# The FFN's gate and up projections as seven half-width block products

## The chip, the cores and the metric

The kernel runs on one core of one Trainium2 chip. The metric is the device time of one execution in microseconds (us). Timed executions are taken without the profiler; the profile is one further execution, taken with it. A core has a matrix engine (PE, with its weight loads shown as PEld), a vector engine (DVE), a scalar engine (ACT), a general engine (POOL, GpSimd) and a sync engine (SP) that issues most transfers. 16 DMA engines move the data. Matrix results land in PSUM, of which this kernel uses eight tiles of 128 partitions x 512 float32; all else on the core lies in SBUF.

## The reference

Two layers of a decoder trunk on x of 512 positions x 1024 channels, all in float32. A layer first mixes tokens (differential attention, retention and a gated short convolution, each projected, gated and summed, then an output projection). Its second half is the FFN:

```
h  = rmsnorm(x, norm_ffn_g)                 # 512 x 1024
gu = h @ w_ffn_in                           # 512 x 5632
g, u = gu[:, :2816], gu[:, 2816:]
g  = conv_b + sum over t = 0..2 of g shifted by 2 - t positions * conv_w[t]
x  = x + (silu(g) * u) @ w_ffn_out          # 2816 -> 1024
```

The FFN's 2816 inner channels are 22 tiles of 128.

## The kernel before, in words

Everything is held transposed: channels on the 128 partitions, the 512 positions along the free axis. x is eight tiles `x[k]` of 128 x 512.

**Three passes for one product.** Float32 operands are split into a high part, rounded to the format the matrix engine reads, and a low part, the rest. `mm3` multiplies hi x hi, hi x lo and lo x hi into one PSUM tile. Weights are split on arrival: `load_w` issues the transfer on SP's queue, `split_w` copies the high part on ACT and subtracts on DVE. Both stand in `tc.high_priority()` blocks.

**FFN.** `xg` are the splits of x times the norm's gain; the norm's factor per position, `rB`, is multiplied in after the product. For each tile f, `project` runs 8 k-blocks x 3 passes = 24 matmuls of 512 columns for g and 24 for u. DVE reads g from PSUM times `rB` into `pad`, `conv` makes the convolution with one ACT and two DVE instructions, silu is a Tanh on ACT and a DVE instruction, u is multiplied in, and `split2` makes `act[f]`. Tiles come in groups of 8, 7 and 7. After a group, eight rows d multiply its `act` tiles by `w2` (3 matmuls of 512 columns for each tile and row) and add to `x[d]`.

**Buffers.** Tiles of one tag share slots; a writer waits until an earlier tile of that slot has been read for the last time. Tag "N" has ten slots of 4 KB a partition: in the mixing part it holds values, queries, keys, normalised inputs and the branch inputs `om`; later it holds `y` and `act`. Tag "main" has four PSUM tiles for projections, "aux" four for the rest. `raw` has two slots; split weights of over 512 columns have three, of up to 512 two.

**Mixing part.** `head_chunk(h)` projects head h's q, k and v into the four "main" tiles; their evacuation writes `nat` and `v` (tag N). `attention(h)` turns `nat` into `q` and `k` (tag N) and runs scores, softmax and values through "aux". Gate projections (`side`) are interleaved with it by `weave`. `gate(0, d)` and `branch` follow, then `y` and the output projection.

**Order.** Each engine runs its queue in order. The program order is the order of the Python code; at build time a scheduler puts each engine's instructions in order by priority (program order, high-priority blocks first) on a simulated timeline, taking an instruction when its inputs and its slot are ready there.

Of the kernel before, what the change touches and what calls it, by code (L numbers as in the profile page):

```python
# [20 lines left out]
P = 128  # L21
# [8 lines left out]
GROUPS = (8, 7, 7)  # L30
# [8 lines left out]
FILL = 96  # L39
# [3 lines left out]
HL = 3  # L43

# [6 lines left out]
def trunk(ctx, tc, xT, wr, wh, wt, wda, wret, wsc, wo, wf, w2, par, lamp, relb, onehot, mask, rope, gtab, out):  # L51
# [6 lines left out]
    sp = ctx.enter_context(tc.tile_pool(name="sp", bufs=4))  # L58
    pm = ctx.enter_context(tc.tile_pool(name="pm", bufs=4, space=PSUM))
# [6 lines left out]
    def gslot(name):  # L66
        return tp.tile([P, S], F32, tag="g", name=name, bufs=9)

    def pairN(name):
        return tp.tile([P, 2, S], F32R, tag="N", name=name, bufs=10)  # L70

    def pairA(name, w=S):
        return tp.tile([P, 2, w], F32R, tag="aT", name=name, bufs=2, padded_shape=[P, 2, S])

    def wide(name, dt=F32R):
        return tp.tile([P, ST, 256], dt, tag="N", name=name, bufs=10)
# [33 lines left out]
    def main(name):  # L110
        return pm.tile([P, S], F32, tag="main", name=name)
# [6 lines left out]
    def ordered(i):  # L118

        if starting[0]:  # L120
            tc.keep_in_program_order(i)
        return i

    def load_w(src, name):
        n = src.shape[1]
        with tc.high_priority():
            raw = wp.tile([P, n], F32, tag="raw", bufs=2, name="raw_" + name, padded_shape=[P, D])
            ordered(nc.sync.dma_start(raw, src))
        return raw

    def split_w(raw, name):
        n = raw.shape[1]
        with tc.high_priority():
            tag, bufs = ("", HL) if 2 * n > D else ("b", 2)
            hi, lo = [
                wp.tile([P, n], F32R, tag=t + tag, name=f"{t}_{name}", padded_shape=[P, D if n > D // 2 else D // 2], bufs=bufs)
                for t in ("hi", "lo")
            ]
            A.copy(hi, raw)  # L139
            V.tensor_tensor(lo, raw, hi.bitcast(F32), ALU.subtract)  # L140
        return hi, lo
# [4 lines left out]
    def mm3(o, a, b, start, stop):  # L146

        T.matmul(o, a[0], b[0], start=start, stop=False)  # L148
        T.matmul(o, a[0], b[1], start=False, stop=False)  # L149
        T.matmul(o, a[1], b[0], start=False, stop=stop)  # L150
# [20 lines left out]
    xs = [cp.tile([P, 2, S], F32R, name=f"xs{k}") for k in range(KT)]  # L171
    klz = cp.tile([P, 2, S], F32R, name="klz")
    state = cp.tile([P, 2, ST - 1, P], F32R, name="state")
    qz = [cp.tile([P, ST, 2, P], F32R, name=f"qz{a}") for a in range(2)]
    rope_t = cp.tile([P, 2, ST, 64], F32, name="rope_t")
    mask_t = cp.tile([P, P], F32, name="mask_t")
    bias_t = cp.tile([P, H, S], F32, name="bias_t")
# [19 lines left out]
    def constants():  # L197
        for l in range(1, DEPTH):
            nc.sync.dma_start(pars[l], par[l])
        nc.sync.dma_start(gtab_t, gtab)  # L200
        nc.sync.dma_start(rope_t, rope)
        nc.sync.dma_start(mask_t, mask)

    def biases():

        rb = cp.tile([BUCKETS + 1, 16], F32, name="rb")[:, :H]
        V.memset(rb[BUCKETS : BUCKETS + 1], -BIG)
        G.dma_start(rb[:BUCKETS], relb)
        line = dr.tile([H, 640], F32, name="line")
        for a, b in ((0, 512), (512, 640)):  # L210
            oh = temp(f"oh{a}", b - a)[: BUCKETS + 1]
            G.dma_start(oh, onehot[:, a:b])
            ps = aux(f"psb{a}")
            T.matmul(ps[:H, : b - a], rb, oh, start=True, stop=True)
            row = temp(f"line{a}", b - a)[:H]
            V.tensor_copy(row, ps[:H, : b - a])
            G.dma_start(line[:, a:b], row)
        skew = dr.tile([H, P * 640], F32, name="skew")
        G.dma_start(skew.rearrange("h (p n) -> h p n", n=640), line.unsqueeze(1).broadcast_to([H, P, 640]))
        src = skew[:, 127 : 127 + 639 * P].rearrange("h (p n) -> p h n", n=639)  # L220
        G.dma_start(bias_t, src[:, :, :S])
# [5 lines left out]


    G.memset(state.bitcast(F32), 0.0)

    G.memset(klz.bitcast(F32), 0.0)
    for t in qz:
        G.memset(t.bitcast(F32), 0.0)
# [11 lines left out]
    def split_x(l, which, name, k):  # L245

        return split2(x[k], xs[k], pars[l][:, which + k : which + k + 1])
# [48 lines left out]
    def layer(l):  # L296
        pt = pars[l]
        L = f"L{l}"
        lam_init = 0.8 - 0.6 * math.exp(-0.3 * l)
# [56 lines left out]
        if not l:  # L356
            for _ in range(3 - STATS):
                next(first)
            constants()
        r, rB = norm_x(f"m{L}")  # L360
# [13 lines left out]
        if not l:  # L374
            biases()

# [52 lines left out]
        def attention(h):  # L429
# [22 lines left out]
            o = sp.tile([P, S], F32, tag="o", name=f"o{h}{L}", bufs=2)  # L452
# [265 lines left out]


        xg = [split_x(l, G_FFN, f"f{L}", k) for k in range(KT)]  # L720
        rB = None
        f0 = 0
        for grp, width in enumerate(GROUPS):
            act = []
            for fi in range(width):
                f = f0 + fi
                ps = main(f"pg{f}{L}")
                project(xg, ps, weights(wf[l, 2 * f], f"fg{L}{f}"))
                if rB is None:
                    _, rB = norm_x(f"f{L}")  # L730
                padt = pads[f % 2]
                V.tensor_tensor(padt[:, 2 : S + 2], ps, rB, ALU.mult)
                c = temp(f"c{f}{L}")
                wc = FF_W + 3 * f
                conv(c, padt, lambda t: pt[:, wc + t : wc + t + 1], pt[:, FF_B + f : FF_B + f + 1])
                th = temp(f"fth{f}{L}")
                A.activation(th, c, AF.Tanh, scale=0.5)
                V.scalar_tensor_tensor(c, th, 1.0, c, ALU.add, ALU.mult)
                ps = main(f"pu{f}{L}")
                project(xg, ps, weights(wf[l, 2 * f + 1], f"fu{L}{f}"))  # L740
                u = temp(f"u{f}{L}")
                V.tensor_tensor(u, ps, rB, ALU.mult)
                V.tensor_tensor(u, u, c, ALU.mult)
                at = pairN(f"act{f}{L}")
                act.append(split2(u, at))
            for d in range(KT):
                w = weights(w2[l, d, :, f0 * P : (f0 + width) * P], f"w2{L}{grp}{d}")
                ps = main(f"p2{grp}{d}{L}")
                project(act, ps, w)
                V.scalar_tensor_tensor(x[d], ps, 0.5, x[d], ALU.mult, ALU.add)  # L750
                if l == DEPTH - 1 and grp == len(GROUPS) - 1:
                    nc.sync.dma_start(out[:, d], x[d])
            f0 += width
# [37 lines left out]
def _layout(i):  # L791
# [28 lines left out]
    wf = i["w_ffn_in"].reshape(DEPTH, KT, P, 2, FT, P).transpose(0, 4, 3, 2, 1, 5)  # L820
    a["wf"] = C(wf).reshape(DEPTH, 2 * FT, P, KT * P)
# [40 lines left out]
```

## Time and profile before

| | |
|---|---|
| median of 3 runs | 1549.39 us (1548.54 to 1551.32) |
| the profiled execution | 1548.07 us |
| its span, first to last instruction | 1546.0 us |
| granted PE clock | 1.000 |
| PE busy | 1538.0 us |
| DVE busy | 980.2 us |
| ACT busy | 625.3 us |
| transfers | 147.04 MB |

The profile names a group of instructions by line, engine and operation, with output <- inputs; a number that tells tiles of one kind apart is left out of some names, and the last letter is the layer without its number, so one row often stands for both layers (x2: one in each). Shapes are partitions x elements. "Idle before" is the time the engine stood still ahead of the group, and what ended it. In the timeline a row begins with its start and its length in us. Matmuls are pipelined: one of 512 columns is shown 0.39 us long and the next starts sooner than that. The view of one tile gives shortest, median and longest duration in ns and the first and last start.

### The profile page before, as it was taken

How to read it: one execution, taken by the hardware profiler on the slowest of the kernel's cores; microseconds unless marked ns; L12 is line 12 of the kernel's file. 1: busy time of each engine (PE TensorE's matmuls, PEld its weight loads, DVE VectorE, ACT ScalarE, POOL GpSimd, SP SyncE). 2: the span in 40 equal slices, each digit the busy share in tenths (PEclk: the TensorE clock that was granted, in tenths of full speed). 3: DMA queues.
4: the chain of work that ended last, by engine and by line, in shares of the span. 5: the costliest groups of instructions: out<-in, count | busy, mean ns of one | idle time of the engine just before them, and what ended most of it. 6: DMA issues, size and time to landing. Idle time of an engine off the chain costs nothing.

```text
span 1546.0 us, 18968 instructions
## 1 busy us (share of the span) xinstructions
PE 1538.0 (99%) x7286; PEld 1304.6 (84%) x7286; DVE 980.2 (63%) x1826; ACT 625.3 (40%) x1057; POOL 10.0 (1%) x22
## 2 busy tenths in 40 slices
PE   9999999999999999999999999999999999999998
PEld 7899988888888888888889999888888888888887
DVE  8498886655576456456666887865555763664662
ACT  4456664333343233233425565643333432332331
POOL 1000000000000000000000000000000000000000
PEclk9999999999999999999999999999999999999999
DMA  5332222233233333332322222322323333323323
GB/s 188 120 99 71 76 93 96 75 103 89 96 96 96 96 100 93 97 105 91 100 82 93 72 89 73 96 76 91 101 95 94 96 97 96 96 89 102 96 89 102
DMA packets 46890, 147.04 MB, mean 95 GB/s; under 512 B 6119, under 2 KB 6518, under 8 KB 46800
## 3 DMA queue, kind: packets, MB, share of 16 engines
q1 hardware_dynamic: 45216, 143.11, 29.6%
q0 software_dynamic: 1584, 2.72, 0.6%
q8 instruction: 57, 0.93, 0.3%
q14 instruction: 33, 0.27, 0.1%
HBM read 143.70 MB, written 3.42 MB: 95 GB/s over the span
## 4 chain that ended last, share of the span: by engine, by line
PE 98%; DMA 1%; DVE 0%; ACT 0%; issue 0%; SPq 0%; ACTq 0%; DVEq 0%
PE pnrvgL L150 1%; PE pnrvgL L148 1%; PE pnrvgL L149 1%; PE pnrqkL L149 1%; PE pnrqkL L150 1%; PE pnrqkL L148 1%; PE pnh3L L149 1%; PE pnh1L L148 1%; PE pnh2L L150 1%; PE pnh3L L148 1%; PE pnh2L L148 1%; PE pnh1L L150 1%; PE pnh2L L149 1%; PE pnh1L L149 1%; PE pnh3L L150 1%; PE pnh0L L148 1%
## 5 line engine op out<-in xcount | busy, mean ns | idle before, releaser
L139 ACT CAST hi_tL<-raw_tL 128x1024 fp32r<-128x1024 f32 x60 | 63.0, 1050 | 124.5 <-DMA raw_tL<-in_wt 24.5
L139 ACT CAST hi_fuL<-raw_fuL 128x1024 fp32r<-128x1024 f32 x44 | 46.4, 1054 | 149.8 <-issue 17.5
L139 ACT CAST hi_w2L<-raw_w2L 128x896 fp32r<-128x896 f32 (+1 forms) x48 | 47.1, 982 | 139.8 <-PE p220L L149 11.8
L140 DVE TENSOR_TENSOR lo_tL<-raw_tL,hi_tL 128x1024 fp32r<-128x1024 f32 x60 | 73.4, 1224 | 16.8 <-ACT hi_tL L139 16.2
L139 ACT CAST hi_fgL<-raw_fgL 128x1024 fp32r<-128x1024 f32 x44 | 46.3, 1053 | 79.2 <-issue 13.0
L140 DVE TENSOR_TENSOR lo_fuL<-raw_fuL,hi_fuL 128x1024 fp32r<-128x1024 f32 x44 | 53.9, 1225 | 26.8 <-ACT hi_fuL L139 26.8
L140 DVE TENSOR_TENSOR lo_w2L<-raw_w2L,hi_w2L 128x896 fp32r<-128x896 f32 (+1 forms) x48 | 54.4, 1134 | 4.0 <-ACT hi_w2L L139 2.3
L140 DVE TENSOR_TENSOR lo_fgL<-raw_fgL,hi_fgL 128x1024 fp32r<-128x1024 f32 x44 | 53.7, 1220 | 3.5 <-ACT hi_fgL L139 3.5
L139 ACT CAST hi_oL<-raw_oL 128x1024 fp32r<-128x1024 f32 x16 | 16.9, 1054 | 56.4 <-PE ptg7L L149 13.1
L149 PE MATMUL pnrqkL<-lo_nrqkL,xs 128*128 128x512 f32 x64 | 25.2, 394 | 0.1
L150 PE MATMUL pnrvgL<-hi_nrvgL,xs 128*128 128x512 f32 x64 | 25.1, 392 | 0.0
L149 PE MATMUL pnrvgL<-lo_nrvgL,xs 128*128 128x512 f32 x64 | 25.0, 391 | 0.0
L150 PE MATMUL pnrqkL<-hi_nrqkL,xs 128*128 128x512 f32 x64 | 24.8, 390 | 0.0
L159 DVE SCALAR_TENSOR_TENSOR xs<-x,par,xs 128x512 fp32r<-128x512 f32 x32 | 23.9, 746 | 1.1 <-ACT xs L158 1.1
L148 PE MATMUL pnrqkL<-hi_nrqkL,xs 128*128 128x512 f32 x64 | 23.5, 403 | 0.9 <-ACT hi_nrqkL L139 0.9
L158 ACT ACTIVATE xs<-x,par 128x512 fp32r<-128x512 f32 x32 | 23.0, 718 | 3.0 <-DMA x<-in_xT 3.0
L148 PE MATMUL pnrvgL<-hi_nrvgL,xs 128*128 128x512 f32 x64 | 23.7, 394 | 0.0
L149 PE MATMUL pnh3L<-lo_nh3L,xs 128*128 128x384 f32 x64 | 22.1, 346 | 0.0
L140 DVE TENSOR_TENSOR lo_oL<-raw_oL,hi_oL 128x1024 fp32r<-128x1024 f32 x16 | 19.6, 1225 | 4.0 <-ACT hi_oL L139 4.0
L150 PE MATMUL pnh2L<-hi_nh2L,xs 128*128 128x384 f32 x64 | 21.9, 343 | 0.0
L149 PE MATMUL pnh2L<-lo_nh2L,xs 128*128 128x384 f32 x64 | 21.7, 339 | 0.0
L148 PE MATMUL pnh1L<-hi_nh1L,xs 128*128 128x384 f32 x64 | 21.7, 338 | 0.0
(3621 smaller groups left out, 5014.0 us busy)
## 6 DMA issues: line engine op xcount, KB each, us to landing
raw_tL<-in_wt SPq DMA_DIRECT2D x60, 512.0 KB, 3.6
raw_fgL<-in_wf SPq DMA_DIRECT2D x44, 512.0 KB, 3.5
raw_fuL<-in_wf SPq DMA_DIRECT2D x44, 512.0 KB, 3.5
raw_w2L<-in_w SPq DMA_DIRECT2D x32, 448.0 KB, 3.2
raw_oL<-in_wo SPq DMA_DIRECT2D x16, 512.0 KB, 3.6
raw_w2L<-in_w SPq DMA_DIRECT2D x16, 512.0 KB, 3.4
raw_nrvgL<-in_wr SPq DMA_DIRECT2D x8, 512.0 KB, 3.6
raw_bdL<-in_wda SPq DMA_DIRECT2D x16, 256.0 KB, 2.6
```

The lines of the kernel that those rows point to most:

```text
L139: A.copy(hi, raw)
L140: V.tensor_tensor(lo, raw, hi.bitcast(F32), ALU.subtract)
L148: T.matmul(o, a[0], b[0], start=start, stop=False)
L149: T.matmul(o, a[0], b[1], start=False, stop=False)
L150: T.matmul(o, a[1], b[0], start=False, stop=stop)
L158: A.activation(hi, src, AF.Copy, scale=g)
L159: V.scalar_tensor_tensor(lo, src, g, hi.bitcast(F32), ALU.mult, ALU.subtract)
```

## The change

The first group has five tiles and stays as it was but for silu, now one ACT instruction (`plain`); the other 17 tiles of a layer (groups of 9 and 8) go through `seven`. There g and u of one tile are a 2 x 2 block matrix: rows u and g, the two halves of the 1024 input channels as the inner blocks, the two halves of the positions as columns. Seven products of 4 k-blocks x 256 columns replace the eight that a plain computation has, with sums of weight blocks as one operand and sums of x blocks as the other.

The x side is made once per layer by `halves`: x times gain and `rB` for two of the eight k-tiles, two sums and two differences of their halves, and splits of seven blocks into `X[k]`. It is called after tiles 2, 3 and 4 and after row 1 of the first group. The weight side is made for each tile: `raw` holds blocks a11, a22 and a12; `s31` gets a fourth block twice by a transfer on SP, then a transfer on POOL's queue adds two other blocks to it; `s24` is two DVE adds. Splits of these go into `h31`, `l31`, `h24`, `l24`, four of the eight slots that hold `xg` in the first group (tag "x"), and into the weight slots (`w11`, `w2212`). The products share PSUM tiles a and b, which ACT and DVE read between products. Since X holds the norm, `seven` needs no `rB`. The convolution, silu and the product with u are as in `plain`.

Buffers: tag "N" has nine slots instead of ten; `raw` slots grow from 1024 to 1536 columns. Tables, gate slots and similar tiles of the mixing part lie in a pool that exists only there, X and the sums in one that exists only in the FFN, so `rope` and `bias` are loaded in each layer. In the group of nine a row's weights come in two pieces.

```diff
-GROUPS = (8, 7, 7)
+GROUPS = (5, 9, 8)
+HALF = S // 2
+NN = 9
...
     def pairN(name):
-        return tp.tile([P, 2, S], F32R, tag="N", name=name, bufs=10)
+        return tp.tile([P, 2, S], F32R, tag="N", name=name, bufs=NN)
...
+    def slotX(name):
+        return tp.tile([P, 2, S], F32R, tag="x", name=name, bufs=KT)
...
-            raw = wp.tile([P, n], F32, tag="raw", bufs=2, name="raw_" + name, padded_shape=[P, D])
+            raw = wp.tile([P, n], F32, tag="raw", bufs=2, name="raw_" + name, padded_shape=[P, 3 * S])
...
     def layer(l):
+        with tc.tile_pool(name=f"mix{l}", bufs=1, reuse_waits="tile", side="right") as mp:
+            phase[0] = mp
+            mix(l, mp)
+        with tc.tile_pool(name=f"ffn{l}", bufs=1, reuse_waits="tile", side="right") as fp:
+            ffn(l, fp)
...
+        def halves(k):
+            n = []
+            for j in (k, k + KT // 2):
+                t = temp(f"xn{j}{L}")
+                V.scalar_tensor_tensor(t, x[j], pt[:, G_FFN + j : G_FFN + j + 1], norm[0], ALU.mult, ALU.mult)
+                n.append(t)
+            b11, b12, b21, b22 = n[0][:, :HALF], n[0][:, HALF:], n[1][:, :HALF], n[1][:, HALF:]
+            t = sums4(f"xt{k}{L}")
+            V.tensor_tensor(t[:, 0], b11, b12, ALU.subtract)
+            V.scalar_tensor_tensor(t[:, 1], t[:, 0], -1.0, b22, ALU.mult, ALU.subtract)
+            V.tensor_tensor(t[:, 2], b22, b12, ALU.subtract)
+            V.scalar_tensor_tensor(t[:, 3], t[:, 1], -1.0, b21, ALU.mult, ALU.subtract)
+            flat = lambda a: a.rearrange("p a s -> p (a s)")
+            split(b11, X[k][:, 0, 0], X[k][:, 1, 0])
+            split(n[1], flat(X[k][:, 0, 1:3]), flat(X[k][:, 1, 1:3]))
+            split(flat(t), flat(X[k][:, 0, 3:7]), flat(X[k][:, 1, 3:7]))
...
+        def seven(f):
+            both = wf[l, f].rearrange("p (b n) -> p b n", n=S)
+            raw = load_w(wf[l, f, :, S:], f"f{L}{f}")
+            a11, a12 = raw[:, :S], raw[:, 2 * S :]
+            with tc.high_priority():
+                s31 = fp.tile([P, 2, S], F32, tag="sum", name=f"s31{f}{L}", bufs=3)
+                nc.sync.dma_start(s31, both[:, 0:1].broadcast_to([P, 2, S]))
+                G.dma_start(s31, both[:, 1:3], accum_op=ALU.add)
+                w11 = split_w(a11, f"fa{L}{f}")
+                h31, l31 = slotX(f"h31{f}{L}"), slotX(f"l31{f}{L}")
+                split(s31, h31, l31)
+                s24 = fp.tile([P, 2, S], F32, tag="sum", name=f"s24{f}{L}", bufs=3)
+                V.tensor_tensor(s24[:, 0], s31[:, 1], a11, ALU.add)
+                V.tensor_tensor(s24[:, 1], s24[:, 0], a12, ALU.add)
+                h24, l24 = slotX(f"h24{f}{L}"), slotX(f"l24{f}{L}")
+                split(s24, h24, l24)
+                w2212 = split_w(raw[:, S : 3 * S], f"fb{L}{f}")
...
+            def product(o, w, b, start, stop):
+                for k in range(KT // 2):
+                    sl = slice(k * P, (k + 1) * P)
+                    mm3(o, (w[0][:, sl], w[1][:, sl]), (X[k][:, 0, b], X[k][:, 1, b]), start and k == 0, stop and k == KT // 2 - 1, True)
+
+            a = main(f"pa{f}{L}")[:, :HALF]
+            b = main(f"pb{f}{L}")
+            padt = pads[f % 2]
+            u = temp(f"u{f}{L}")
+            product(a, w11, 0, True, True)
+            A.copy(padt[:, 2 : HALF + 2], a)
+            product(b[:, HALF:], (h31[:, 1], l31[:, 1]), 3, True, True)
+            A.copy(u[:, HALF:], b[:, HALF:])
+            product(a, (h24[:, 0], l24[:, 0]), 4, False, True)
+            A.copy(padt[:, HALF + 2 : S + 2], a)
+            product(b[:, HALF:], (h24[:, 1], l24[:, 1]), 2, False, True)
+            product(a, (h31[:, 0], l31[:, 0]), 5, False, True)
+            V.tensor_tensor(u[:, HALF:], u[:, HALF:], a, ALU.add)
+            product(b[:, :HALF], w12, 1, False, True)
+            V.tensor_tensor(padt[:, 2 : S + 2], padt[:, 2 : S + 2], b, ALU.add)
+            product(a, w22, 6, False, True)
+            A.copy(u[:, :HALF], a)
+            c = temp(f"c{f}{L}")
+            wc = FF_W + 3 * f
+            conv(c, padt, lambda t: pt[:, wc + t : wc + t + 1], pt[:, FF_B + f : FF_B + f + 1])
+            A.activation(c, c, AF.Silu)
+            V.tensor_tensor(u, u, c, ALU.mult)
+            return split2(u, pairN(f"act{f}{L}"))
...
+            for f in range(f0, f0 + width):
+                act.append(seven(f) if grp else plain(f))
+                if grp == 0 and f >= 2 and len(todo) > 1:
+                    halves(todo.pop(0))
             for d in range(KT):
+                rows(grp, f0, act, d)
+                if todo and d == 1:
+                    halves(todo.pop(0))
```

More of the change, by code (lines that the diff above doesn't have):

```diff
@@ L38 @@
 SINGLE = 1
-FILL = 96
+FILL = 80
 SOME = 5
@@ L144, in weights, with mm3 @@
         return split_w(load_w(src, name), name)
[L146 to L150, printed above, removed]
+    def mm3(o, a, b, start, stop, more=False):
+        T.matmul(o, a[0], b[0], start=start, stop=False, skip_group_check=more)
+        T.matmul(o, a[0], b[1], start=False, stop=False, skip_group_check=more)
+        T.matmul(o, a[1], b[0], start=False, stop=stop, skip_group_check=more)
     def split(src, hi, lo, g=None):
@@ L200, in constants @@
         nc.sync.dma_start(gtab_t, gtab)
-        nc.sync.dma_start(rope_t, rope)
         nc.sync.dma_start(mask_t, mask)
+    skew = dr.tile([H, P * 640], F32, name="skew")
     def biases():
@@ L296, in layer, with mix, tables @@
     def layer(l):
+        with tc.tile_pool(name=f"mix{l}", bufs=1, reuse_waits="tile", side="right") as mp:
[3 more added lines that the diff above has]
+            ffn(l, fp)
+    def mix(l, mp):
         pt = pars[l]
         L = f"L{l}"
+        klz = mp.tile([P, 2, S], F32R, name=f"klz{L}")
+        state = mp.tile([P, 2, ST - 1, P], F32R, name=f"state{L}")
+        qz = [mp.tile([P, ST, 2, P], F32R, name=f"qz{a}{L}") for a in range(2)]
+        rope_t = mp.tile([P, 2, ST, 64], F32, name=f"rope{L}")
+        bias_t = mp.tile([P, H, S], F32, name=f"bias{L}")
+        G.memset(state.bitcast(F32), 0.0)
+        G.memset(klz.bitcast(F32), 0.0)
+        for t in qz:
+            G.memset(t.bitcast(F32), 0.0)
+        def tables():
+            src = skew[:, 127 : 127 + 639 * P].rearrange("h (p n) -> p h n", n=639)
+            G.dma_start(bias_t, src[:, :, :S])
         lam_init = 0.8 - 0.6 * math.exp(-0.3 * l)
@@ L722, in layer @@
         f0 = 0
+        todo = list(range(KT // 2))
         for grp, width in enumerate(GROUPS):
             act = []
[L725 to L745, printed above, removed]
```

91 lines of the change are left out of this document (58 added, 33 removed).

## The prediction

> **What bounds the kernel now.** I read the page first, then the granted clock, then windows over one group of the feed-forward part (FFN).
>
> ```profile
> span 1546.0 us, 18968 instructions
> ...
> PE 1538.0 (99%) x7286; PEld 1304.6 (84%) x7286; DVE 980.2 (63%) x1826; ACT 625.3 (40%) x1057; POOL 10.0 (1%) x22
> ...
> PE 98%; DMA 1%; DVE 0%; ACT 0%; issue 0%; SPq 0%; ACTq 0%; DVEq 0%
> ```
>
> ```profile
> core 0: us, PE busy (x) PEld busy (x) DVE busy (x) ACT busy (x) POOL busy (x), PEclk, DMA share, GB/s
> 1318.00:1389.00 71.00, 71.00 (x314) 58.79 (x314) 46.63 (x59) 26.71 (x33) 0.00 (x0) 1.00 0.31 95
> 1389.00:1432.00 43.00, 43.00 (x191) 35.64 (x190) 17.48 (x20) 9.46 (x10) 0.00 (x0) 1.00 0.33 98
> ```
>
> The chain that ended last is 98% PE, and in both stages of a group (the first window makes `act` tiles, the second multiplies them by `w2`) PE is busy all the time at full clock, with no wait left to remove. So only less PE work shortens this kernel, and any wait that the change puts on PE is paid in full. A busy PE says nothing about its rate; for that I take steps from start to start.
>
> ```profile
> L148 PE MATMUL pg9L<-xs,hi_fgL x16: 389/389/389, 559.2 to 1328.9; 128*128 128x512 f32 x16
> ...
> L148 PE MATMUL pg10L<-xs,hi_fgL x16: 389/389/389, 570.1 to 1339.8; 128*128 128x512 f32 x16
> ```
>
> ```profile
> 1320.55 0.39 PE L150 MATMUL pu8L<-xs,lo_fuL 128*128 128x512 f32 x1
> 1320.55 0.19 PEld L148 LDWEIGHTS pu8L<-xs,hi_fuL 128*128 128x128 f32 x1
> 1320.78 0.39 PE L148 MATMUL pu8L<-xs,hi_fuL 128*128 128x512 f32 x1
> ```
>
> ```profile
> 73.71 0.28 PE L148 MATMUL pS01L<-qz,rT2L 128*128 128x256 f32 x1
> ...
> 74.31 0.28 PE L150 MATMUL pS01L<-qz,rT2L 128*128 128x256 f32 x1
> ```
>
> One FFN tile (g and u, 48 matmuls of 512 columns) takes 570.1 - 559.2 = 10.9 us, 0.227 us a matmul. The retention scores are six matmuls of 256 columns in a row: (74.31 - 73.71) / 5 = 0.120 us a step. So half the width costs 53% of the time, and each step has about 13 ns that don't shrink (2 x 0.120 - 0.227).
>
> **The change, part by part.** Five of the 22 tiles of a layer stay plain; 17 become seven products.
>
> *PE, seven products.* Each is 4 k-blocks x 3 passes = 12 matmuls of 256 columns, so a tile is 84 x 0.120 = 10.08 us instead of 48 x 0.227 = 10.88: 0.80 us less, 34 tiles in two layers, **-27.2 us**. The 12.5% fewer columns become 7%, since the 13 ns come 84 times instead of 48. That 0.120 holds for a long run, too, rests on the weight load: four transposes of 128 columns, each with a load of its own, take 0.44 us, 110 ns each,
>
> ```profile
> 169.44 0.44 PE pto0L L288 x4
> ```
>
> so loads can follow each other at least that fast, just under 120. Between 0.110 and 0.125 a step the term is -55 to -13 us; I take 0.120, measured at this width. The `w2` matmuls keep their number and width.
>
> *Vector and scalar work per tile.* The nearest rows:
>
> ```profile
> L140 DVE TENSOR_TENSOR lo_fgL<-raw_fgL,hi_fgL 128x1024 fp32r<-128x1024 f32 x44 | 53.7, 1220 | 3.5 <-ACT hi_fgL L139 3.5
> L139 ACT CAST hi_fgL<-raw_fgL 128x1024 fp32r<-128x1024 f32 x44 | 46.3, 1053 | 79.2 <-issue 13.0
> ```
>
> ```profile
> L139 ACT CAST hi_bdL<-raw_bdL x16: 604/623/624, 294.1 to 1121.5; 128x512 fp32r<-128x512 f32 x16
> L140 DVE TENSOR_TENSOR lo_bdL<-raw_bdL,hi_bdL x16: 682/684/685, 295.4 to 1122.3; 128x512 fp32r<-128x512 f32 x16
> ```
>
> ```profile
> L600 ACT COPY onr1L<-por11L x2: 374/374/374, 113.6 to 878.5; 128x256 f32<-128x256 f32 x2
> L601 DVE TENSOR_TENSOR onr1L<-onr1L,por11L x2: 420/421/422, 114.0 to 878.9; 128x256 f32<-128x256 f32 x2
> ```
>
> ```profile
> L294 DVE SCALAR_TENSOR_TENSOR c9L<-pad,par,c9L 128x512 f32<-128x512 f32 x1 | 0.8, 753 | 0.0
> ...
> L743 DVE TENSOR_TENSOR u8L<-u8L,c8L 128x512 f32<-128x512 f32 x1 | 0.7, 693 | 0.0
> ```
>
> ```profile
> L292 ACT ACTIVATE c9L<-pad,par 128x512 f32<-128x512 f32 x1 | 0.8, 812 | 0.0
> ...
> L737 ACT ACTIVATE fth9L<-c9L 128x512 f32<-128x512 f32 x1 | 0.6, 631 | 2.0 <-DVE c9L L294 2.0
> ```
>
> DVE: low part of `w11` 0.68; of `s31`, `s24` and `w2212` 3 x 1.22; the two adds for `s24` 2 x 0.69; `u+=a` 0.42; `pad+=b` 0.69; the convolution 2 x 0.75; `u*c` 0.69; low part of `act` 0.68. Sum 9.70 us in 10.08, where the window above has 46.63 / 71.00 of it. ACT: 0.62 + 3 x 1.05 + four PSUM copies 4 x 0.37 + 0.81 + Silu (not in the trace; 0.63 as the Tanh) + 0.62 = 7.31 us. DVE fits, because independent instructions overlap:
>
> ```profile
> 1319.80 1.22 DVE L140 TENSOR_TENSOR lo_fuL<-raw_fuL,hi_fuL 128x1024 fp32r<-128x1024 f32 x1 [0.17 <-ACT hi_fuL L139]
> 1320.94 0.74 DVE L293 SCALAR_TENSOR_TENSOR c8L<-pad,par,c8L 128x512 f32<-128x512 f32 x1
> ```
>
> 1.22 long, but the next starts after 1.14; eight such pairs bring 9.70 to about 9.1. That lies beside PE, with 1 us to spare per tile, and two tiles' worth of weight slots as a cushion. On average it costs nothing; if the cover were gone (PE waiting for all of DVE's surplus) the price is the last rival.
>
> *Hand-offs inside a tile.* All seven products go through two PSUM tiles, so PE waits at four places for a reader: products 3, 4 and 5 for ACT copies, product 7 for DVE's `u+=a`. Between comes one product, 12 x 0.120 = 1.44 us. A result lands 0.28 - 0.12 = 0.16 us after its step, the copy is 0.37 (DVE 0.42): about 0.8 us remain for whatever stands ahead on the engine, and that is a weight split of 1.05 (ACT) or 1.22 (DVE) marked high priority. Bounds: nothing, if no split stands in front; (1.22 - 0.8) + 3 x (1.05 - 0.8) = 1.2 us if one does each time. Big splits fill 3.15 / 10.08 of ACT's time and only the first quarter of each hurts, so nearer to nothing: 0.1 us a tile, **+3.4 us** (0 to 40).
>
> *Ten N slots become nine.* The mixing phase before the FFN uses all ten. From the views of single tiles:
>
> ```profile
> L155 ACT CAST oms0L<-scy0L x2: 612/612/612, 106.6 to 870.8; 128x512 fp32r<-128x512 f32 x2
> ...
> L148 PE MATMUL pb22L<-oms0L,hi_b2L x2: 402/402/402, 205.6 to 970.6; 128*128 128x512 f32 x2
> ```
>
> ```profile
> L158 ACT ACTIVATE om0L<-pto0L,par x2: 689/689/689, 169.9 to 934.9; 128x512 fp32r<-128x512 f32 x2
> ```
>
> ```profile
> L501 PE MATMUL po22L<-v2L,aT23L x8: 330/332/338, 232.4 to 998.2; 128*128 128x256 f32 x8
> ```
>
> ```profile
> L158 ACT ACTIVATE v3L<-pnh3L,rmL x8: 366/370/390, 202.6 to 971.6; 128x128 fp32r<-128x128 f32 x8
> ```
>
> ```profile
> L465 PE MATMUL pS022L<-k2L,q2L x2: 427/427/427, 204.8 to 969.8; 128*128 128x384 f32 x2
> ...
> L465 PE MATMUL pS123L<-k2L,q2L x2: 448/448/448, 216.3 to 981.3; 128*128 128x512 f32 x2
> ```
>
> At 203 us the branch inputs `oms0`, `oms1`, `omr0`, `omr1` are held, `om0` too, head 2's `v2`, `q2`, `k2`, and `nat3`; `v3` is the tenth. With nine it can't be written until `q2` and `k2` are free, at 216.3 in this order. Until then all four main PSUM tiles hold head 3's projection, and the gate projections queued behind it on PE stop. Bounds per layer: 0, if another slot is free by then, to 216.3 - 204.8 = 11.5 us. Without the gates PE reaches the last scores of head 2 sooner, so I take 3 us a layer, **+6 us**. The other full stretches delay only attention tiles that gate matmuls cover.
>
> *Group ends and starts.* The first `w2` row needs the group's last `act` at once: with eight in a group PE has 21 matmuls (4.8 us) before it, with five only 12 (2.7 us). The plain tail behind PE is 0.69 + 0.69 + 0.62 + 0.68 = 2.7 us and some gaps; the seven-product tail is longer (0.37 or 0.69, 0.81, 1.50, 0.63, 0.69, 0.62, 0.68, part of it under product 7: some 4 us against 5.4 or 4.8 of cover), and the next tiles' splits (5.7 us of DVE) push in with priority. `halves` adds some 5.6 us of DVE four times in the first group. Bounds 0 to 5 us a layer; **+3.4 us** for both layers together.
>
> *Transfers.* Per tile 768 KB of weights, 512 KB for `s31`, and 512 KB that add to it, 1.8 MB against 1.0.
>
> ```profile
> raw_fgL<-in_wf SPq DMA_DIRECT2D x44, 512.0 KB, 3.5
> ...
> bias_t<-skew POOLq DMA_DIRECT2D x1, 1024.0 KB, 5.8
> skew<-line POOLq DMA_DIRECT2D x1, 1280.0 KB, 19.4
> ```
>
> Share 0.31 now, so 0.6 of the 16 engines, and 0.75 if adding doubles its half MB. No row has an adding transfer: between 3.5 us (a plain one) and 19.4 us (the slowest of POOL's); I take 6. It waits for the plain transfer on POOL's queue, where in the FFN nothing stands behind it. 3.5 + 6 us end well inside the two tiles (20 us) by which `s31` can run ahead: 0 on the path. What POOL's queue gets besides (a second bias load, memsets) comes tens of us before use: 0, as do the second `rope` load on SP and the strided plain weights.
>
> *Sum* against the profiled execution (1548.07, span 1546.0 and 2.1 around): -27.2 + 3.4 + 6 + 3.4 = -14.4. The median of the runs is 1.3 above that execution; from it, 1549.4 - 14.4 = **1535 us**.
>
> **The rivals.**
>
> *Full gain.* Waits and slots cost nothing: 1549.4 - 27.2 = 1522. For it: PE has no idle stretch today, and queues are ordered for readiness. Against it: 9.1 us of DVE in 10.08, and the tenth slot in use.
>
> *Slower: DVE and ACT as the pace of the seven products.* Place: the four hand-offs. If queues put one big split before each and DVE, late, pushes the next tile's splits into the next hand-offs, a tile loses the 1.2 us above: 34 x 1.2 = 41, with the other terms 1549.4 - 27.2 + 41 + 9 = 1572. It decides from (27.2 - 9.4) / 34 = 0.52 us a tile upwards. For it: DVE goes from 66% to over 90%. Against it: ACT has a quarter of its time free.
>
> *No change.* Slots at their upper bound (23 us for both layers) and hand-offs as forecast: 1549.4 - 27.2 + 23 + 3.4 = 1549.
>
> *Adding transfers set the pace.* `s31` and `s24` share three buffers; with about 5 us for `s24` and 5 for the splits, an adding transfer above some 17 us ((3.5 + 17 + 5 + 5) / 3 = 10.2) makes `s31` late. At 19.4 a tile takes (3.5 + 19.4 + 5 + 5) / 3 = 11.0 us, 0.9 more: 1549.4 - 14.4 + 34 x 0.9 = 1566.
>
> *A weight load that doesn't overlap.* Then each half-width matmul would take 0.110 + 0.120 and a tile 84 x 0.23 = 19.3 us: 1549.4 + 34 x 8.4 = 1835. The rows speak against it: the load at 1320.55 starts together with a matmul, and the step is 0.227, not 0.110 longer. The Trainium skill, "TensorE: Matmul & The Clock Gate", in the part on packing small matmuls ("The mechanism"), says that a weight load overlaps matmuls in flight only when their row group differs; by that rule this rival would be the forecast, and this trace does not agree.
>
> **How the numbers follow.** Forecast 0.52 (1527 to 1544), full gain 0.16, no change 0.10, DVE and ACT 0.18, adding transfers 0.03, load 0.01. The range for 8 in 10 leaves out the upper part of the slower cases: 1521 to 1558. Less than 0.2% (3.1 us) can't be told from none here. Faster: 0.52 + 0.16 and a part of the no-change case, 0.70; same, the rest of that case, 0.08; slower 0.18 + 0.03 + 0.01 = 0.22.
>
> **What would show it.** Seven-product tiles with 84 matmuls, 10.1 us from tile to tile when undisturbed; a step near 0.120. Gaps on PE ahead of products 3, 4, 5, 7, ended by ACT copies or `u+=a`; a gap near 205 and 970 us ended by `v3`; gaps at the first `w2` row. DVE above 85% in those windows, DMA share near 0.6, and adding transfers that land in under 10 us. Wrong would be: a step above 0.125, tiles above 10.6 us, PE waiting for `h31`, or no gap at `v3`.

## The result, and the profile after

| | before | after |
|---|---|---|
| median of the runs | 1549.18 us (1548.54 to 1551.32) | 1636.78 us (1630.98 to 1642.64) |
| the profiled execution | 1548.07 us | 1636.98 us |
| span | 1546.0 us | 1635.2 us |

The ratio is 1.0563, 95% interval 1.0542 to 1.0584: slower by 5.6%. The forecast was 1535 us, and the time lies far outside its range.

From the page of after: the span, PE's busy time, the granted clock in 40 slices, the DMA share in the same slices, and the chain of work that ended last.

```profile
span 1635.2 us, 22053 instructions
...
PE 1556.4 (95%) x8510; PEld 1369.2 (84%) x8510; DVE 1066.0 (65%) x2006; ACT 734.6 (45%) x1304; POOL 43.2 (3%) x61
...
PEclk9999989999999999989999999999999999998899
DMA  5422212232225752652422222222323366426623
...
PE 73%; DMA 12%; DVE 7%; issue 5%; ACT 3%; SPq 0%; POOLq 0%; ACTq 0%; DVEq 0%
```

The chain that was 98% PE now runs through transfers for 12% and DVE for 7%. PE's own time splits the loss. Idle PE went from 1546.0 - 1538.0 = 8.0 us to 1635.2 - 1556.4 = 78.8 us: 70.8 more. Busy PE grew by 18.4 us although the products should have taken 27.2 off it: 45.6 more for the same matmuls. The mean granted clock of after is 0.973, and 0.027 x 1635 = 44 us of clock are missing, though some of the half-clock time is idle time too. So of the 70.8 + 45.6 = 116.4 us lost (27.2 of them made good by the products) some 60% is waiting, and most of the rest is PE running at half clock after it waited.

By stage, from windows of after (span, busy time and count of each engine, granted clock, DMA share, GB/s; the stages are mixing, plain tiles, their `w2` rows, the group of nine with its rows, the group of eight with its rows) and, below, of before (mixing and FFN). Layer 0 alone is shown; in layer 1 the mixing stage loses 11.2 us and the FFN some 7 us more than here, in the same stages.

```profile
6.00:427.60 421.60, 412.79 (x2039) 353.75 (x2039) 284.99 (x654) 196.05 (x391) 4.61 (x7) 0.99 0.30 97
427.60:483.40 55.80, 55.80 (x253) 46.33 (x252) 41.71 (x70) 26.32 (x34) 0.00 (x0) 1.00 0.25 82
483.40:516.40 33.00, 29.40 (x121) 23.09 (x121) 24.95 (x40) 13.09 (x19) 0.92 (x1) 0.95 0.49 138
516.40:672.10 155.70, 145.78 (x973) 136.09 (x972) 98.42 (x133) 70.60 (x115) 8.49 (x10) 0.97 0.54 143
672.10:817.80 145.70, 132.31 (x865) 122.32 (x864) 91.27 (x121) 68.00 (x107) 9.25 (x11) 0.94 0.46 126
```

```profile
6.00:416.30 410.30, 407.55 (x2039) 351.60 (x2039) 286.90 (x654) 197.32 (x391) 4.59 (x7) 1.00 0.32 100
416.30:776.80 360.50, 360.50 (x1598) 298.58 (x1596) 211.48 (x273) 123.19 (x151) 0.00 (x0) 1.00 0.31 96
```

The mixing stage is 421.6 - 410.3 = 11.3 us longer. The FFN takes 390.2 us instead of 360.5 (817.8 - 427.6), where 346.9 were expected (17 tiles x 0.80 us less): 43 us too many, in the two groups of seven-product tiles and the rows ahead of them. The plain tiles are undisturbed.

What PE waits for in 672 to 775 us of after, and what DVE waits for in 505 to 775 us (us in total, times, longest). DVE's first row is twelve waits for splits of `w2`, the longest 3.7 us; the rows behind it are the adds for `s24`:

```profile
PE pa14L L159 <- DVE u14L L828: 6.0, 1, 6.0
PE pa19L L159 <- DVE pad L830: 2.7, 1, 2.7
PE pa20L L159 <- DVE pad L830: 1.9, 1, 1.9
```

```profile
DVE lo_w2L L151 <- ACT hi_w2L L150: 18.4, 12, 3.7
DVE s2417L L804 <- DMA s3117L<-in_wf: 6.6, 1, 6.6
DVE s2420L L804 <- issue: 5.6, 1, 5.6
DVE s2416L L804 <- DMA s3116L<-in_wf: 5.2, 1, 5.2
```

PE waits for DVE to read a PSUM tile, but DVE is not busy: it waits for an adding transfer. (For tile 20 the profile names no releaser; the adding transfer is issued at 724.0 us and lands 6.8 us later, when the wait ends.) DVE's queue in order of time shows the rest:

```profile
686.84 1.22 DVE L167 TENSOR_TENSOR l3116L<-s3116L,h3116L 128x1024 fp32r<-128x1024 f32 x1
687.97 0.68 DVE L830 TENSOR_TENSOR pad<-pad,pb14L 128x512 f32<-128x512 f32 x1
695.24 0.69 DVE L804 TENSOR_TENSOR s2417L<-s3117L,raw_fL 128x512 f32<-128x512 f32 x1 [6.58 <-DMA s3117L<-in_wf]
695.85 0.41 DVE L828 TENSOR_TENSOR u14L<-u14L,pa14L 128x256 f32<-128x256 f32 x1
```

The next product on PE is the seventh of tile 14, and it needs `u14 += a`. But the first add for `s24` of tile 17 stands in DVE's queue *ahead of* that read. The add waits 6.58 us for its transfer; the 0.41 us read behind it waits as long. The same on ACT puts a split of `s31` of tile 5 ahead of the splits of `w2` at 489 us (it waits 6.53 us), which lengthens the rows of the first group.

The transfer is late because its chain begins late. The two issues for tile 17, on SP and on POOL, and the instruction that releases the first:

```profile
676.25 1.22 DVE L167 TENSOR_TENSOR l2415L<-s2415L,h2415L 128x1024 fp32r<-128x1024 f32 x1
```

```profile
677.50 0.38 SPq L798 DMA_DIRECT2D s3117L<-in_wf  x1
```

```profile
685.88 0.85 POOL L799 DMA_DIRECT2D s3117L<-in_wf  x1 [9.14 <-DVE lo_faL L151]
```

With three "sum" buffers and two a tile, `s31` of tile f takes the buffer of `s24` of tile f - 2. The transfer starts when that is split (676.25 + 1.22 = 677.47). The first transfer lands 7.8 us after its issue (the row of the second names a DVE instruction that ends shortly after), the second 9.3 after its own, and the sum is there 17.7 us after the start, at 695.2. These two are the slowest pair of the 17 tiles; the medians are 5.7 and 7.0. With the splits the next release, `l2417`, comes 28.2 us after `l2415`, where two tiles of PE's work are 20.2.

### The profile page after: what moved, and what is told of

It is laid out like the page before. It is cut to its first block, busy times and chain, and to the rows that moved or that the text cites. A ratio compares the mean times of both kernels' runs of the same rounds, so it can differ in the third digit from the quotient of the medians.

```text
span 1635.2 us, 22053 instructions
## 1 busy us (share of the span) xinstructions
PE 1556.4 (95%) x8510; PEld 1369.2 (84%) x8510; DVE 1066.0 (65%) x2006; ACT 734.6 (45%) x1304; POOL 43.2 (3%) x61
## 2 busy tenths in 40 slices
DMA packets 61433, 175.30 MB, mean 107 GB/s; under 512 B 6951, under 2 KB 7350, under 8 KB 61328
## 4 chain that ended last, share of the span: by engine, by line
PE 73%; DMA 12%; DVE 7%; issue 5%; ACT 3%; SPq 0%; POOLq 0%; ACTq 0%; DVEq 0%
DMA raw_w2L<-in_w 2%; DMA s317L<-in_wf 2%; DMA s3115L<-in_wf 2%; DMA s3116L<-in_wf 1%; DMA s3117L<-in_wf 1%; PE pnrvgL L161 1%; PE pnrvgL L159 1%; DMA s3111L<-in_wf 1%; DMA s315L<-in_wf 1%; PE pnrvgL L160 1%; PE pnrqkL L160 1%; PE pnrqkL L161 1%; PE pnrqkL L159 1%; DVE lo_w2L L151 1%; PE pnh2L L161 1%
## 5 line engine op out<-in xcount | busy, mean ns | idle before, releaser
L150 ACT CAST hi_w2L<-raw_w2L 128x640 fp32r<-128x640 f32 (+2 forms) x64 | 49.4, 781 | 107.7 <-DMA raw_w2L<-in_w 43.3
L151 DVE TENSOR_TENSOR lo_w2L<-raw_w2L,hi_w2L 128x640 fp32r<-128x640 f32 (+2 forms) x64 | 56.4, 889 | 50.6 <-ACT hi_w2L L150 50.5
L151 DVE TENSOR_TENSOR lo_tL<-raw_tL,hi_tL 128x1024 fp32r<-128x1024 f32 x60 | 73.4, 1224 | 19.6 <-ACT hi_tL L150 19.4
L150 ACT CAST hi_fbL<-raw_fL 128x1024 fp32r<-128x1024 f32 x34 | 35.6, 1048 | 26.8 <-DMA raw_fL<-in_wf 15.5
L151 DVE TENSOR_TENSOR lo_fbL<-raw_fL,hi_fbL 128x1024 fp32r<-128x1024 f32 x34 | 41.5, 1222 | 6.8 <-ACT hi_fbL L150 6.7
L150 ACT CAST hi_faL<-raw_fL 128x512 fp32r<-128x512 f32 x34 | 21.0, 618 | 34.9 <-DMA raw_fL<-in_wf 32.3
L151 DVE TENSOR_TENSOR lo_fuL<-raw_fuL,hi_fuL 128x1024 fp32r<-128x1024 f32 x10 | 12.2, 1225 | 19.6 <-ACT hi_fuL L150 19.6
L150 ACT CAST hi_fuL<-raw_fuL 128x1024 fp32r<-128x1024 f32 x10 | 10.5, 1050 | 31.1 <-issue 12.0
L151 DVE TENSOR_TENSOR lo_faL<-raw_fL,hi_faL 128x512 fp32r<-128x512 f32 x34 | 23.4, 687 | 0.4 <-ACT hi_faL L150 0.4
L150 ACT CAST hi_fgL<-raw_fgL 128x1024 fp32r<-128x1024 f32 x10 | 10.5, 1053 | 24.1 <-issue 16.0
L151 DVE TENSOR_TENSOR lo_fgL<-raw_fgL,hi_fgL 128x1024 fp32r<-128x1024 f32 x10 | 12.2, 1222 | 2.2 <-ACT hi_fgL L150 2.2
```

The lines of the kernel that those rows point to most:

```text
L150: A.copy(h, raw)
L151: V.tensor_tensor(w, raw, h.bitcast(F32), ALU.subtract)
```

## The experiments

Two theories for the FFN. *Late sums*: the two transfers in a row, released late, hold DVE and ACT in front of the PSUM readers queued behind. *Pace*: DVE (9.7 of 10.08 us a tile) and ACT are simply full, the prediction's slower rival. A third would be the traffic itself, 175.30 MB against 147.04. Besides them: too few buffers, which is why the sums are late, and for the mixing stage the nine slots. Edits are against the kernel after unless said otherwise; the ratio is to the kernel before.

**Nine slots alone** (against the kernel before):

```diff
-        return tp.tile([P, 2, S], F32R, tag="N", name=name, bufs=10)
+        return tp.tile([P, 2, S], F32R, tag="N", name=name, bufs=9)
...
-        return tp.tile([P, ST, 256], dt, tag="N", name=name, bufs=10)
+        return tp.tile([P, ST, 256], dt, tag="N", name=name, bufs=9)
```

> The kernel before with nine N slots in place of ten and nothing else changed. The kernel after has 11.3 and 11.2 us more than before in its two mixing stages, with PE idle near 205 and 1011 us. If the missing slot does that by itself, this run takes 1549 + 22 = 1571 us (1565 to 1577). By the prediction (3 us a layer) it takes 1555. If the second bias load, the memsets and the scoped pools do it, it stays at 1549.

1571.69 us (1.0149, 1.0133 to 1.0164): 23.6 us more than the 1548.0 of before on that chip, as much as the two mixing stages of after lose (11.3 + 11.2). From the view of one tile and from windows of this run:

```profile
L158 ACT ACTIVATE v3L<-pnh3L,rmL x8: 360/368/380, 218.2 to 995.4; 128x128 fp32r<-128x128 f32 x8
```

```profile
203.00:224.00 21.00, 16.25 (x59) 12.40 (x59) 16.45 (x63) 12.41 (x42) 0.00 (x0) 0.68 0.24 74
```

`v3` is first written at 218.2 us, 202.6 before. In the 21 us around it PE is idle for 4.7 and runs at a mean clock of 0.68.

**The same slots, relieved** in the kernel after:

```diff
-            nat = wide(f"nat{h}{L}", F32)
+            nat = mp.tile([P, ST, 256], F32, tag="nat", name=f"nat{h}{L}", bufs=2)
```

> The kernel after with attention's nat tiles in two buffers of the mixing phase's own pool, so that the nine N slots have two users fewer at a time. If the nine slots are the whole of the 22.5 us that the mixing stages lost, those stages come back to 410 and 404 us and the run takes 1637 - 22.5 = 1614 us (1608 to 1620). If the pools, the second bias load or the clock did it, 1637.

1614.18 us (1.0429, 1.0403 to 1.0455), 22.6 less than after. The other parts of the scoped pools, and the second load of `rope` and `bias`, cost nothing that shows.

**The transfers, one or two, plain or adding.** The first edit reads two blocks with one plain transfer, the second makes both transfers plain. Both leave the addition out, so `s31` and `s24` hold other values and the output is not the FFN's; the work on the engines stays.

```diff
-                nc.sync.dma_start(s31, both[:, 0:1].broadcast_to([P, 2, S]))
-                G.dma_start(s31, both[:, 1:3], accum_op=ALU.add)
+                nc.sync.dma_start(s31, both[:, 1:3])
```

> The kernel after, with s31 read by one plain transfer in place of the plain and the adding one (the addition is left out, so s31 and s24 hold other values; every instruction of DVE, ACT and PE stays). Late sums: if the adds and splits that wait for the adding transfer hold up the PSUM readers queued behind them, most of the 67 us that the two seven-product stages and the w2 rows lost beyond the forecast go away, and this takes 1549 - 27 + 23 (mixing) + 5 to 25 = 1550 to 1570 us. Pace of DVE and ACT: their work is the same, so it stays between 1620 and 1637.

```diff
-                G.dma_start(s31, both[:, 1:3], accum_op=ALU.add)
+                G.dma_start(s31, both[:, 1:3])
```

> The kernel after, with the second transfer of s31 plain too: the same two queues, the same order, the same bytes written, but nothing is added on the way (the sum is left out of the computation). If it is the two transfers in a row that make s31 late, this stays near the kernel after, 1610 to 1637 us. If it is the adding that is slow (7 us against 3.5 to 5 for a plain 512 KB), it takes 1570 to 1600. Pace of DVE and ACT: 1637.

1553.58 us (1.0035, 1.0024 to 1.0046) with one plain transfer, 1585.30 (1.0241, 1.0210 to 1.0271) with two plain ones, 1636.78 as it is. All three run the same number of instructions on DVE, ACT and PE. The DMA issues of tile 10 (KB each, median us from issue to landing), in the order one plain, two plain, after:

```profile
s3110L<-in_wf SPq DMA_DIRECT2D x2, 512.0 KB, 3.8
```

```profile
s3110L<-in_wf SPq DMA_DIRECT2D x2, 512.0 KB, 4.6
s3110L<-in_wf POOLq DMA_DIRECT2D x2, 512.0 KB, 4.7
```

```profile
s3110L<-in_wf SPq DMA_DIRECT2D x2, 512.0 KB, 5.7
s3110L<-in_wf POOLq DMA_DIRECT2D x2, 512.0 KB, 6.7
```

Over the 17 tiles the medians are 3.7, 4.9 + 4.4 and 5.7 + 7.0 us. The time follows the length of that chain: 3.7, 9.3, 12.7 us to the sum; 1554, 1585, 1637 us. Late sums, then, and neither half alone: the second transfer costs 32 us, its adding 51 more. The pace theory, which expected no change, falls. The run with one transfer also moves less (157.46 MB), so the traffic is not ruled out yet; the run with two plain ones moves as much as after and still gains 51 us.

**The queues' order.** Sums and splits of tile f are traced under a block that queues what it holds behind the given instructions on their engines:

```diff
+        def late(f):
+            n = f - group[0]
+            if n < 2:
+                return w2s[n - 2]
+            return ends[f - 2]
...
-            with tc.high_priority():
-
+            with tc.high_priority(), ExitStack() as queued:
+                for i in late(f):
+                    queued.enter_context(tc.issue_after(i))
...
+            ends[f] = (end_v.ins, end_a.ins)
```

Here `end_v` is `pad += b`, `end_a` the copy of `u`'s lower half, and `w2s` holds the splits of the rows of `w2`.

> The kernel after with its two transfers, but the weight sums and splits of tile f are queued on DVE and ACT behind the last PSUM readers of tile f-2 (behind the last w2 splits for the first two tiles of a group). Late sums: a late transfer then can hold up only the readers of tile f-1, and the 6 us gaps go; 1565 to 1600 us. Pace of DVE and ACT: the same work in a stiffer order, 1637 or more.

1589.12 us (1.0269, 1.0252 to 1.0286). PE's 6 us pause ahead of tile 14's seventh product is gone, but transfers are still late (DVE's waits for adding transfers in the window 480 to 790 us, the largest whose releaser the profile names):

```profile
DVE s246L L817 <- DMA s316L<-in_wf: 5.6, 1, 5.6
DVE s2415L L817 <- DMA s3115L<-in_wf: 4.6, 1, 4.6
DVE s249L L817 <- DMA s319L<-in_wf: 3.9, 1, 3.9
```

**The buffers.** `s24` is written over `s31`, so the transfers of tile f wait for tile f - 3 (the two halves of `s24` change places, and so do the products that read them):

```diff
-                s24 = fp.tile([P, 2, S], F32, tag="sum", name=f"s24{f}{L}", bufs=3)
-                V.tensor_tensor(s24[:, 0], s31[:, 1], a11, ALU.add)
-                V.tensor_tensor(s24[:, 1], s24[:, 0], a12, ALU.add)
+                V.tensor_tensor(s31[:, 1], s31[:, 1], a11, ALU.add)
+                V.tensor_tensor(s31[:, 0], s31[:, 1], a12, ALU.add)
...
-                split(s24, h24, l24)
+                split(s31, h24, l24)
...
```

> The kernel after with s24 written over s31 once s31 is split, so that a tile uses one sum buffer in place of two and the transfers of tile f wait for tile f-3 in place of f-2; the order of the queues is left to the planner. Too few buffers as the cause: 1570 to 1600 us. Order of the queues as the cause: sums are queued as early as before, now a tile further ahead; 1600 to 1637.

1578.65 us (1.0190, 1.0175 to 1.0206), 58 less than after with no order by hand. The largest waits of DVE in its group of nine are

```profile
DVE lo_faL L151 <- ACT hi_faL L150: 6.3, 5, 2.5
DVE lo_w2L L151 <- ACT hi_w2L L150: 6.0, 5, 2.5
DVE x L850 <- PE p206L L161: 2.7, 1, 2.7
```

and none of DVE's waits there is for an adding transfer. What ACT waits for most in the same window is the tiles' plain weights (`raw`, 22.6 us in 8 waits), and the waits of `lo_fa` hang on them. Starting the transfers a tile sooner helped more (58 us) than hiding their lateness in the queue (48 us).

**Together, and the floor.**

> Three edits together: sums and splits queued behind the readers of tile f-2, s24 in place of s31, nat in the mixing phase's pool. Late sums: transfers now have a tile more, so no DVE or ACT instruction should wait for one, and the remaining cost is hand-offs and group starts: 1549 - 27 + 3 (group ends) + 5 to 25 = 1530 to 1550 us. Pace of DVE and ACT: 1549 - 27 + 41 + 9 = 1572 or more.

1549.31 us (1.0004, 0.9995 to 1.0014): no different from before, at the upper end of what was expected. It moves 175.29 MB, as much as after, and takes 87 us less: the traffic by itself is not the cause.

> The kernel after with s31 read by one plain transfer (the addition left out) and nat in the mixing phase's pool: both losses taken away, the products, copies, sums and splits all there. If the two losses are independent and there is no third, 1553.6 - 22.5 = 1531 us (1527 to 1536), near the forecast's own sum without its slot term (1549.4 - 27.2 + 3.4 + 3.4 = 1529).

1529.38 us (0.9874, 0.9851 to 0.9897); again the addition is left out. The two losses add: alone they give back 83.2 and 22.6 us, together 107.4. This is 7.2 us above the prediction's full gain (1549.4 - 27.2 = 1522.2), or 8.5 counted from the 1548.1 of before on this chip. One window inside its group of nine:

```profile
525.00:585.00 60.00, 60.00 (x503) 60.00 (x502) 51.06 (x72) 38.72 (x65) 0.00 (x0) 1.00 0.31 104
```

PE never stops for 60 us, 60.00 / 503 = 0.119 us a matmul (those that reach in at the edges are counted, so 0.119 to 0.120), with DVE 85% busy.

In order_in_place_nat PE still waits for the prepared weights themselves (480 to 790 us):

```profile
PE pa5L L162 <- ACT hi_faL L152: 2.7, 1, 2.7
PE pb19L L162 <- ACT h3119L L169: 1.0, 1, 1.0
PE pb21L L162 <- ACT h3121L L169: 1.0, 1, 1.0
PE pb17L L162 <- ACT h3117L L169: 1.0, 1, 1.0
```

Queueing that work earlier, against order_in_place_nat (`f0s` is `group`; `w2s` has one entry a row in the first group and two in the second):

```diff
-                return w2s[n - 2]
+                return w2s[(n - 4) * (1 if f0s[0] < 6 else 2)]
...
-            A.copy(padt[:, HALF + 2 : S + 2], a)
+            end_a = A.copy(padt[:, HALF + 2 : S + 2], a)
...
-            V.tensor_tensor(u[:, HALF:], u[:, HALF:], a, ALU.add)
+            end_v = V.tensor_tensor(u[:, HALF:], u[:, HALF:], a, ALU.add)
```

> As order_in_place_nat, but the sums and splits of tile f are queued one or two products earlier (behind the second pad copy and u += a of tile f-2), and those of the first two tiles of a group behind the splits of the fourth- and third-last rows of w2. Over there PE still waits 1.1 us for h31 in every second tile and about 4 us at a group's start: with those gone 1549 - 10 = 1539 us (1534 to 1545). If it is no better, 1549, the waits come from DVE's and ACT's load and not from where the queue puts them.

1537.75 us (0.9922, 0.9903 to 0.9941): the wait for `hi_fa` of tile 5 falls from 2.7 to 0.2 us and those for `h31` are gone, so they were of the queue's making. This version computes the whole FFN, has the adding transfer in it, and takes 0.8% less than the kernel before.

**No adding transfer.** All four blocks come in one transfer, and an engine adds (the rest as in order_in_place_nat, without its order, with two "sum" buffers; for dve_adds `V` in place of `G`):

```diff
-            raw = load_w(wf[l, f, :, S:], f"f{L}{f}")
+            raw = load_w(wf[l, f], f"f{L}{f}")
...
-                nc.sync.dma_start(s31, both[:, 0:1].broadcast_to([P, 2, S]))
-                G.dma_start(s31, both[:, 1:3], accum_op=ALU.add)
+                r4 = raw.rearrange("p (b n) -> p b n", n=S)
+                G.tensor_tensor(s31, r4[:, 1:3], r4[:, 0:1].broadcast_to([P, 2, S]), ALU.add)
```

> All four weight blocks of a tile come in one plain transfer of 1 MB, GpSimd makes s31 in one add of 128x1024, s24 is written in place of s31, nat has its own pool; no adding transfer, no order by hand. Late sums: s31 is ready a few us after its weights, and what is left is near the plain run without the mixing cost: 1527 to 1550 us. If GpSimd's add takes long (over 7 us) or slows DVE beside it, 1560 to 1620.

> As pool_adds, with the 128x1024 add on DVE: no adding transfer, no GpSimd, one DVE instruction of about 1.2 us more a tile, so 9.1 + 1.1 = 10.2 to 10.9 us of DVE in a tile of 10.08. Late sums: nothing is late, 1530 to 1548 us. Pace of DVE: DVE is now over the tile's time, and the tile grows to DVE's 10.2 to 10.9 us and its hand-offs: 1545 to 1575.

1562.43 us (1.0086, 1.0071 to 1.0102) with GpSimd, 1536.21 (0.9916, 0.9898 to 0.9933) with the same add on DVE. From the groups of the GpSimd run (busy us, mean ns): the add itself at its shortest and longest, and DVE's low part of `w11`, then the same row of after:

```profile
L799 POOL TENSOR_TENSOR s3113L<-raw_fL 128x1024 f32<-128x1024 f32 x2 | 8.0, 3986 | 17.4 <-DVE u10L L827 17.4
...
L799 POOL TENSOR_TENSOR s3116L<-raw_fL 128x1024 f32<-128x1024 f32 x2 | 4.7, 2374 | 17.1 <-DMA raw_fL<-in_wf 17.1
```

```profile
L151 DVE TENSOR_TENSOR lo_faL<-raw_fL,hi_faL 128x512 fp32r<-128x512 f32 x34 | 48.0, 1411 | 11.3 <-ACT hi_faL L150 11.3
```

```profile
L151 DVE TENSOR_TENSOR lo_faL<-raw_fL,hi_faL 128x512 fp32r<-128x512 f32 x34 | 23.4, 687 | 0.4 <-ACT hi_faL L150 0.4
```

DVE's subtract for `w11` takes on average twice as long in the run with GpSimd's adds. One of each that meet, in order of time:

```profile
519.46 2.40 POOL L799 TENSOR_TENSOR s318L<-raw_fL 128x1024 f32<-128x1024 f32 x1 [3.55 <-DVE l246L L167]
519.58 3.37 DVE L167 TENSOR_TENSOR l317L<-s317L,h317L 128x1024 fp32r<-128x1024 f32 x1
```

The subtract takes 3.37 us where one that meets no add takes 1.22 (`l246`, 518.11). With the add on DVE the kernel is 26 us faster, although DVE has more to do; how much of this is the meeting and how much the add's own 2.37 to 3.99 us, by which `s31` is later, was not separated. A window of dve_adds:

```profile
525.00:585.00 60.00, 60.00 (x498) 59.75 (x497) 56.23 (x75) 39.44 (x66) 0.00 (x0) 1.00 0.27 93
```

DVE is 94% busy, and PE still never waits. That is the second count against the pace theory: with more DVE work than after has (1103.0 us against 1066.0) this kernel is faster than after by 100 us, and than before by 12.

> As dve_adds, with the queue order of order_early. If order helps when DVE is full, below dve_adds by 5 to 15 us; if DVE's time alone sets the tile, the same within 3 us.

1548.30 us (0.9998, 0.9988 to 1.0008), 12 us more than dve_adds, which neither expectation had: one saw a gain, the other no change. With nothing late, the order by hand is a loss here. Which of its constraints costs this was not taken apart.

## Why the prediction was wrong

*Seven products on PE, -27.2 us*: right. The step is 0.119 us over 60 us in a row, a weight load with each matmul, and in plain_s31_nat PE's busy time is 24.1 us below before (1538.0 - 1513.9). The rival of a load that doesn't overlap is out.

*Vector and scalar work, 0*: right. It fits at 85% and at 94% of DVE, on both sides of the prediction's 9.1 of 10.08 us (90%). The slower rival built on it named the right place (PSUM readers behind something on DVE's queue) and the wrong cause: DVE was held by a wait, not by work.

*Transfers, "0 on the path"*: **the step that failed**, worth 83 us. The size was near: an adding transfer landed after 7.0 us in the median (6 taken, bounds 3.5 and 19.4), the plain one ahead of it after 5.7 (3.5 taken), and DMA was busy 0.61 of 516 to 620 us as expected. Wrong was "end well inside the two tiles (20 us) by which `s31` can run ahead". Two tiles is what the eight "x" slots hold, at four splits a tile. But the "sum" buffers let the transfers begin only after tile f - 2's last split, so transfers, adds and splits lie in one chain that must go round in two tiles, 20.2 us. With the prediction's own sizes (3.5 + 6 for the transfers, 5 for `s24`, 5 for the splits) that chain is 19.5 us, with no time to spare; with the measured 5.7 + 7.0 the same estimate gives 22.7. The rival on adding transfers had the same mistake: it divided the buffers' total holding time by three, as if they could be held in any order, and came to a threshold of 17 us, where the chain gives 20.2 - 3.5 - 5 - 5 = 6.7. In `order_in_place_nat` the same transfers have a tile more time, and none of DVE's waits is for an adding transfer any more.

Also missed: who stands behind the waiting instruction. The prediction says that nothing stands behind the adding transfer on POOL's queue, and never asked it of the adds and splits that wait for it. On DVE and ACT the PSUM readers stand there, of tile 14 behind an add of tile 17. Why the scheduler put them so can't be seen in a trace; that it took the transfers for shorter than they are is the likely reason, only argued here.

*Hand-offs, +3.4, and group ends, +3.4*: the sum is right, 7.2 to 8.5 us in plain_s31_nat, where nothing is late; the places are not, so part of this is luck. There PE waits for hand-offs at tile 5 alone (2.1 us over both layers, where 0.1 us in each of 34 tiles was forecast), and for the `w2` rows in the fourth and fifth (2.5 us) and not in the first. PE's idle time is 4.9 us above before (1526.8 - 1513.9 against 8.0); the rest is the 3.1 us by which its busy time misses the 27.2. In after the longest pause lies at a hand-off that was named, ahead of product 7, with another cause; others are ended by `pad += b`, which was not named.

*Ten N slots become nine, +6*: mechanism and place right, the size wrong. It took 23.6 us by itself, just above the upper bound of 2 x 11.5. `v3` waited as described: it starts at 218.24 us, when the last matmul with `k2` (217.47, 0.73 long) has ended. The argument that PE then reaches the last scores sooner didn't hold: that matmul starts 1.2 us later than in the kernel before. Between 203 and 219 us the kernel before puts 38 gate matmuls (`ptg`) between attention's, nine_slots none, and without them attention's own waits lie open. So PE's gaps there are ended by attention, not by `v3` as the prediction had it; PE's waits in 195 to 235 us of nine_slots, none of which the kernel before has there:

```profile
PE po02L L501 <- ACT aT20L L155: 1.9, 1, 1.9
PE pto1L L288 <- DVE o1L L522: 1.4, 1, 1.4
```

And the stall was charged at full clock, where the window above has a mean of 0.68.

## What to carry to other kernels

An instruction that waits for a transfer delays everything behind it in its engine's queue, as the add for tile 17 did. So a transfer "off the path" must be followed to its first reader, and then to whoever stands behind that reader in its queue. A prefetch distance is the smallest over all the buffers in its chain: find for each buffer which earlier tile's last read releases it, and compare the length of the whole chain, not a landing time, with the tiles between. Where a stall is priced on a busy PE, price the slower clock that can follow it too: here 70.8 us more of idle PE came with 45.6 us more of busy time.

## What was not expected of the hardware

**A pause of PE can cost more than its length.** In the run with one plain transfer PE is undisturbed up to one pause, then (PE in order of time, and windows behind it):

```profile
516.33 0.28 PE L161 MATMUL pa6L<-X3L,lo_faL 128*128 128x256 f32 x1
519.08 0.39 PE L159 MATMUL pa5L<-X0L,h245L 128*128 128x256 f32 x1 [2.48 <-ACT pad L820]
```

```profile
517.00:520.20 3.20, 1.12 (x9) 1.12 (x10) 3.20 (x4) 3.01 (x6) 0.00 (x0) 1.00 0.77 260
520.30:523.60 3.30, 3.30 (x18) 3.30 (x17) 2.36 (x4) 0.26 (x2) 0.00 (x0) 0.50 0.36 130
```

After 2.48 us without work the clock is 0.50 for some 3.4 us, although PE is working again: 14 matmuls begin between 520.66 and 523.44 us, 0.214 us apart and not 0.120. So this pause cost some 1.5 us beyond its length. In nine_slots the clock is 0.50 for 12 us, from 212 to 224, after and between pauses of 0.7 to 1.9 us. But the 2.7 us pause of order_in_place_nat ahead of tile 5, which ends at 504.6, brings no such stretch in this layer:

```profile
504.60:588.00 83.40, 82.17 (x678) 81.56 (x679) 73.72 (x99) 53.93 (x90) 6.79 (x8) 1.00 0.64 171
```

So the length of a pause does not decide it alone; what else does is not shown here. The Trainium skill, "TensorE: Matmul & The Clock Gate", "What's actually happening", describes a free-running window of about 3.4 us after which an idle PE is slowed to half; the 3.4 us of the slow stretch agree. Its rule under "Why this matters for your kernels", to avoid idle gaps above some 3 us, is too generous by these rows: 2.48 us was enough once, and shorter pauses in a row were in nine_slots.

**GpSimd beside DVE.** The add of 128x1024 takes 2.37 to 3.99 us, and a DVE subtract of two SBUF tiles that meets it took 3.37 us in place of 1.22. The Trainium skill, "SBUF — State Buffer", "Who interferes with whom", says that a DVE instruction with two SBUF inputs contends with a GpSimd instruction that reads SBUF; these rows agree.
